# Routing one-hots stored with two tokens innermost, spilled activations read back into their ring ahead of use, gate table read in quarters

## The chip, the cores and the metric

The kernel runs on one NeuronCore of a Trainium2 chip. The metric is the device time of one execution, in microseconds (us). The kernel before takes 1592.83 us, the median of three runs between 1591.17 and 1601.28 us.

## What is computed

The reference is one decoder layer on 512 tokens of width 1024: attention and a convolution branch, then a retrieval layer ("PEER") over 16,384 single-neuron experts, then a gated embedding. The change lies in the PEER layer, whose core is:

```
def one_block(xb):
    q = (xb @ w_q).reshape(P, PEER_HEADS, 2, PEER_DK_HALF)
    s = jnp.einsum('phcd,hcnd->phcn', q, sub_keys).astype(jnp.float32)
    v1, i1 = lax.top_k(s[:, :, 0], PEER_TOPK)
    v2, i2 = lax.top_k(s[:, :, 1], PEER_TOPK)
    ...
    best, pos = lax.top_k(cand, PEER_TOPK)
    e = jnp.take_along_axis(cand_idx, pos, axis=-1)
    g = jax.nn.softmax(best, axis=-1)
    u = u_tab[e]
    act = jax.nn.gelu(jnp.einsum('pd,phkd->phk', xb, u).astype(jnp.float32), approximate=False)
    coef = (g * act).astype(xb.dtype)
    return jnp.einsum('phk,phkd->pd', coef, v_tab[e])
```

Each token chooses 8 x 16 = 128 of the 128 x 128 experts, each with a gate g. The expert number is i1 * 128 + i2.

## The kernel before

The 512 tokens are four groups of 128. The first group fetches its chosen experts' rows by indirect DMA (`gathered`: 128 rows of u, lines 802 and 806, then 128 rows of v, lines 813 and 816, each 512 KB for 128 tokens). The other three groups, 384 tokens, go through all 16,384 experts densely and are multiplied with a table of gates that is zero where an expert was not chosen. The dense work is 128 units of each of two kinds:

- An **A unit** e (`prep_act`, `dense_act`) loads 128 experts of u (tile `tr`, 512 KB), splits them into a high and a low part (`th` on ScalarE, `tl` on VectorE, the helper at lines 135 and 140), does 24 matmuls of 384 columns into `aps` (lines 148 to 150), and takes the GELU into a tile `act` from a ring of RING = 17. The activations of units 0 to 47 (e < SPILL) are written to memory (`ad`), the others stay in the ring.
- A **V unit** e (`prep_out`, `dense_out`) loads 128 experts of v (`tr` again), splits them, multiplies the activations with the gates into `cf` (VectorE, line 1020), splits `cf` into `ch` and `cl`, and does 18 matmuls of 512 columns into `vps`. The gates come from the table `gd` in memory, in chunks of GCH = 8 units: one DMA of 1.5 MB for each chunk, into `gch`, of which two buffers exist (`load_gates`, line 1008).

The order runs in stages. First 65 A units, during which VectorE finds the top keys of the four token groups (`topk`) and, for groups 1 to 3, builds the gate table (the scatter). Then 63 pairs of an A and a V unit, V in the order of `order`: units 48 to 127 first, whose activations are in the ring, then 0 to 47. Then 65 V units alone, the last 48 of which need an activation back from `ad` (tile `aback`, two buffers, loaded where the unit is prepared, line 1015). Units are prepared AHEAD = 2 units before they run; raw tiles `tr` have three buffers, split tiles four. The indirect DMAs and their VectorE work (`gj`, `acc`) are spread over all stages by a fixed rate.

The scatter of one group (`topk`'s end and `scatter`) makes, for every token, a matrix of 128 x 128 gates as a product: for each of the token's 128 choices (the partitions) a one-hot row of i1 and a one-hot row of i2 times the gate, contracted by TensorE. It goes by blocks of OCH = 8 tokens. VectorE compares a ramp `iok` with the indices `ids` (line 937, tile `o12`, the rows' `o`), giving both one-hots for 8 tokens in 2048 f16 elements, and multiplies the second by the gate's high and low half (line 944, `og`, 1024 elements each). TensorE then does two matmuls a token, stationary operand the first one-hot, moving operand `og`, 128 columns (lines 960 and 961, tile `gp`), and ScalarE writes four tokens at a time to `stg` (line 962), which SyncE (SP) stores into `gd`. In memory the tokens of a one-hot lie innermost, in runs of QUAD = 4, since VectorE reads and writes 16-bit elements that lie side by side:

```
o12 = ohp.tile([P, ng, 2, NK, QUAD], F16, name="o12", tag="o12")
nc.tensor.matmul(gp[:, i], o1[:, q // QUAD, :, i], og[:, 0, q // QUAD, :, i], start=True, stop=False)
```

So TensorE reads one token's 128 values at a step of four f16 elements, 8 bytes, in both operands, and VectorE reads the indices of a run (four elements, 8 bytes) once for each of the 128 values of the ramp. The one-hot tiles have two buffers each, and a scatter is issued LATE = 2 blocks after its one-hots.

SP issues nearly all the plain DMAs, in program order; a DMA that waits for a buffer holds those behind it.

Of the kernel before, what the change touches and what calls it, by code (L numbers as in the profile page):

```python
# [9 lines left out]
F32 = mybir.dt.float32  # L10
# [11 lines left out]
P = 128  # L22
# [27 lines left out]
WBUF = 4  # L50
EARLY = 65
# [3 lines left out]
QUAD = 4  # L55
# [38 lines left out]
def hymba_layer(ctx, tc, x, xT, p_t, pos, pvec, conv_ln_g, conv_ln_b, w_in, w_uq, w_ukv, w_out,  # L94
# [724 lines left out]
    with ExitStack() as fs:  # L819
# [9 lines left out]

        iok = mid.tile([P, NK, QUAD], F16, name="iok")  # L830
        nc.gpsimd.iota(iok, pattern=[[1, NK], [0, QUAD]], base=0, channel_multiplier=0,
                       allow_small_or_imprecise_dtypes=True)

        def topk(t):
# [83 lines left out]
            ids = ohp.tile([P, P // QUAD, 2, QUAD], F16, name="ids", tag="ids")  # L918
            nc.scalar.activation(ids, pt[:, 0:2].rearrange("p c (g q) -> p g c q", q=QUAD), AF.Copy)
# [9 lines left out]
            for c in range(P // TCH):  # L929
                stg = s8p.tile([P, NK, TCH], F32, name="stg", tag="s8")  # L930
                for c0 in range(0, TCH, OCH):
                    cs = slice(c * TCH + c0, c * TCH + c0 + OCH)
                    ng = OCH // QUAD
                    gs0 = cs.start // QUAD
                    o12 = ohp.tile([P, ng, 2, NK, QUAD], F16, name="o12", tag="o12")
                    og = ohp.tile([P, 2, ng, NK, QUAD], F16, name="og", tag="og")
                    nc.vector.tensor_tensor(
                        o12.rearrange("p g c n q -> p (g c) n q"),
                        iok.unsqueeze(1).to_broadcast([P, 2 * ng, NK, QUAD]),
                        ids[:, gs0:gs0 + ng].rearrange("p g c q -> p (g c) q").unsqueeze(2)  # L940
                        .to_broadcast([P, 2 * ng, NK, QUAD]), op=ALU.is_equal)
                    yield 1.2, 0.0
                    for part, gate in ((0, gh), (1, gl)):
                        nc.vector.tensor_tensor(  # L944
                            og[:, part], o12[:, :, 1],
                            gate[:, cs].rearrange("p (g q) -> p g q", q=QUAD).unsqueeze(2)
                            .to_broadcast([P, ng, NK, QUAD]), op=ALU.mult)
                    o1 = o12[:, :, 0]
                    late.append((c, c0, stg, o1, og))
                    if len(late) > LATE:  # L950
                        scatter(t, *late.pop(0))
                    yield 1.1, 0.94
# [3 lines left out]
        def scatter(t, c, c0, stg, o1, og):  # L956
            for q in range(0, OCH, QUAD):
                gp = ps_g.tile([P, 4, NK], F32, name="gp", tag="gp")
                for i in range(4):
                    nc.tensor.matmul(gp[:, i], o1[:, q // QUAD, :, i], og[:, 0, q // QUAD, :, i], start=True, stop=False)  # L960
                    nc.tensor.matmul(gp[:, i], o1[:, q // QUAD, :, i], og[:, 1, q // QUAD, :, i], start=False, stop=True)  # L961
# [34 lines left out]
    with ExitStack() as fs:  # L996
# [7 lines left out]
        def load_gates(c):  # L1004
            if len(gch) > 1:
                gch.pop(next(iter(gch)))
            gch[c] = cfp.tile([P, NTC, GCH, TCH], F32, name="gch", tag="gch")
            nc.sync.dma_start(gch[c].rearrange("p c n t -> p c (n t)"),
                              gd[:, :, c * GCH:(c + 1) * GCH, :].rearrange("c p n t -> p c (n t)"))

        def prep_out(e):
            stage(("V", e), v_tab.rearrange("(a b) d -> b a d", b=NK)[e], [P, D])
            if e < SPILL:
                a = cfp.tile([P, TD], F32, name="aback", tag="aback")
                nc.sync.dma_start(a, ad[e])
            else:
                a = acts.pop(e)
# [37 lines left out]
        def prep(u):  # L1055
# [4 lines left out]
            for j in (i, i + GCH - 1):  # L1060
                if j < NK and order[j] // GCH not in gch:
                    load_gates(order[j] // GCH)
# [174 lines left out]
```

## Time and profile before

| | |
|---|---|
| median of three runs | 1592.83 us |
| profiled execution, its time | 1598.58 us |
| its span in the trace | 1596.6 us |
| TensorE matmul (PE) busy | 1537.3 us, 96% |
| VectorE (DVE) busy | 1267.1 us, 79% |
| ScalarE (ACT) busy | 719.7 us, 45% |
| DMA | 386.54 MB, mean 242 GB/s |
| granted TensorE clock, mean | 0.983 |

The profiled execution is 5.75 us longer than the median of the three timed runs. Matmuls are pipelined: the record of one is as long as its passage through the array, so the time that it costs is read from one start to the next, and a busy PE may still be paced by something else. In the views, PE is the matmul, PEld the load of the stationary operand, DVE VectorE, ACT ScalarE, POOL GpSimd, SP SyncE; `L937` is line 937 of the kernel before. The helper's lines 135, 140 and 148 to 150 serve many tiles, so they are read by tile.

### The profile page before, as it was taken

To read this page: it belongs to the slowest core of one execution; us is meant where nothing else is said; L and a number is where in the kernel's file an instruction comes from. 1 tells how busy PE (TensorE), PEld (TensorE's weight loads), DVE (VectorE), ACT (ScalarE), POOL (GpSimd) and SP (SyncE) were. 2 spreads that over 40 slices of the span, in tenths; PEclk is the share of its full clock that TensorE was granted. 3 is DMA by queue.
4 is the path that set the end of the run, shared out by engine and by line. 5 is a ranking of instruction groups with operands and counts; after the bars stand their busy time and mean duration, and the time that the engine had idled before them with its cause. 6 is when DMAs were issued, how large, how long until landed. Compare 5 with 4: busy or idle time off the path is not lost.

```text
span 1596.6 us, 22808 instructions
## 1 busy us (share of the span) xinstructions
PE 1537.3 (96%) x8070; PEld 1361.4 (85%) x8070; DVE 1267.1 (79%) x2614; ACT 719.7 (45%) x1160; POOL 414.2 (26%) x302
## 2 busy tenths in 40 slices
PE   7999999999999999999999999899999999889997
PEld 6888777899899999999999998799988888768876
DVE  5999665699989899758879768697977966777766
ACT  6468864344564653653333323333332433333454
POOL 0000001000000001004545444464544543434100
PEclk9999989999999999999999999999999999999998
DMA  7321124436567666589989998898999899889842
GB/s 221 101 80 54 54 94 168 135 108 200 192 242 241 223 242 216 196 267 388 343 313 346 341 345 278 302 330 310 338 323 343 301 316 310 301 284 316 287 144 92
DMA packets 166913, 386.54 MB, mean 242 GB/s; under 512 B 12560, under 2 KB 81552, under 8 KB 163728
## 3 DMA queue, kind: packets, MB, share of 16 engines
q1 hardware_dynamic: 129360, 249.81, 45.9%
q0 software_dynamic: 36864, 134.23, 23.5%
q8 instruction: 63, 1.03, 0.3%
q10 hardware_dynamic: 576, 1.05, 0.2%
q14 instruction: 50, 0.41, 0.1%
HBM read 343.63 MB, written 41.42 MB: 241 GB/s over the span
## 4 chain that ended last, share of the span: by engine, by line
PE 51%; DVE 18%; DMA 16%; issue 8%; ACT 5%; POOL 2%; SPq 1%; DVEq 0%; POOLq 0%; ACTq 0%
PE aps L149 6%; PE aps L150 6%; PE aps L148 6%; PE vps L149 5%; PE vps L150 5%; PE vps L148 4%; DMA aback<-ad 4%; DVE tl L140 3%; DMA tr<-in_v_tab 3%; DMA gv<-in_v_tab,pidx 3%; DMA gu<-in_u_tab,pidx 3%; PE gp L960 3%; PE gp L961 3%; DVE cacc L304 2%; DMA tr<-in_u_t 2%
## 5 line engine op out<-in xcount | busy, mean ns | idle before, releaser
L135 ACT ACTIVATE th<-tr 128x1024 fp32r<-128x1024 f32 x256 | 270.7, 1058 | 475.4 <-DMA tr<-in_u_t 181.0
L140 DVE SCALAR_TENSOR_TENSOR tl<-tr,th 128x1024 fp32r<-128x1024 f32 x256 | 312.3, 1220 | 92.4 <-ACT th L135 91.3
L148 PE MATMUL aps<-mixh,th 128*128 128x384 f32 x1024 | 347.3, 339 | 1.9 <-ACT act L789 1.9
L150 PE MATMUL aps<-mixh,tl 128*128 128x384 f32 x1024 | 346.2, 338 | 0.0
L149 PE MATMUL aps<-mixl,th 128*128 128x384 f32 x1024 | 345.6, 338 | 0.0
L802 POOL DMA_INDIRECT gu<-in_u_tab,pidx x128 | 174.1, 1360 | 565.1 <-DVE gj L806 383.7
L149 PE MATMUL vps<-tl,ch 128*128 128x512 f32 x768 | 304.2, 396 | 11.6 <-DVE tl L140 11.5
L148 PE MATMUL vps<-th,ch 128*128 128x512 f32 x768 | 302.1, 393 | 6.9 <-ACT th L135 6.9
L150 PE MATMUL vps<-th,cl 128*128 128x512 f32 x768 | 302.8, 394 | 0.0
L813 POOL DMA_INDIRECT gv<-in_v_tab,pidx x128 | 213.9, 1671 | 249.6 <-DVE acc L816 217.8
L148 PEld LDWEIGHTS aps<-mixh,th 128*128 128x128 f32 x1024 | 193.8, 189 | 4.8 <-ACT act L789 2.3
L149 PEld LDWEIGHTS aps<-mixl,th 128*128 128x128 f32 x1024 | 193.5, 189 | 2.4
L150 PEld LDWEIGHTS aps<-mixh,tl 128*128 128x128 f32 x1024 | 193.4, 189 | 0.0
L149 PEld LDWEIGHTS vps<-tl,ch 128*128 128x128 f32 x768 | 145.8, 190 | 44.9 <-DVE tl L140 15.8
L806 DVE SCALAR_TENSOR_TENSOR gj<-gu,xn 128x1024 bf16<-128x1024 f32 x128 | 156.2, 1220 | 29.2 <-DMA gu<-in_u_tab,pidx 27.9
L148 PEld LDWEIGHTS vps<-th,ch 128*128 128x128 f32 x768 | 146.0, 190 | 37.6 <-ACT th L135 8.3
L816 DVE SCALAR_TENSOR_TENSOR acc<-gv,gact,acc 128x1024 f32<-128x1024 f32 x128 | 163.8, 1280 | 17.8 <-DMA gv<-in_v_tab,pidx 17.0
L150 PEld LDWEIGHTS vps<-th,cl 128*128 128x128 f32 x768 | 146.0, 190 | 30.5
L135 ACT ACTIVATE ch<-cf 128x384 fp32r<-128x384 f32 x128 | 66.6, 522 | 170.4 <-DVE cf L1020 79.6
L962 ACT ACTIVATE stg<-gp 128x512 f32<-128x512 f32 x96 | 95.4, 1106 | 50.2 <-PE gp L961 30.8
L960 PE MATMUL gp<-og,o 128*128 128x128 f16 x384 | 93.3, 296 | 1.2 <-DVE og L944 1.1
L961 PE MATMUL gp<-og,o 128*128 128x128 f16 x384 | 89.0, 296 | 0.6 <-DVE og L944 0.6
(301 smaller groups left out, 2230.9 us busy)
## 6 DMA issues: line engine op xcount, KB each, us to landing
tr<-in_u_t SPq DMA_DIRECT2D x128, 512.0 KB, 5.7
tr<-in_v_tab SPq DMA_DIRECT2D x128, 512.0 KB, 6.6
gd<-stg SPq DMA_DIRECT2D x24, 1024.0 KB, 4.8
gch<-gd SPq DMA_DIRECT2D x16, 1536.0 KB, 15.8
ad<-act SPq DMA_DIRECT2D x48, 192.0 KB, 3.9
aback<-ad SPq DMA_DIRECT2D x48, 192.0 KB, 5.6
wr<-in_gate_w SPq DMA_DIRECT2D x12, 512.0 KB, 3.3
wr<-in_w_out SPq DMA_DIRECT2D x8, 512.0 KB, 3.2
```

The costliest lines, as they stand in the source:

```text
L135: nc.scalar.activation(hi, src, AF.Copy)
L140: nc.vector.scalar_tensor_tensor(lo, src, 1.0 if g is None else g, hi.bitcast(F32), op0=ALU.mult, op1=ALU.subtract)
L148: nc.tensor.matmul(ps, lh, rh, start=first, stop=False)
L149: nc.tensor.matmul(ps, lh, rl, start=False, stop=False)
L150: nc.tensor.matmul(ps, ll, rh, start=False, stop=last)
L802: nc.gpsimd.indirect_dma_start(out=g, out_offset=None, in_=u_tab, in_offset=bass.IndirectOffsetOnAxis(ap=pidx[:, s:s + 1], axis=0))
L806: nc.vector.scalar_tensor_tensor(junk, g, 1.0, xn0, op0=ALU.mult, op1=ALU.mult, accum_out=gact[:, s:s + 1]))
L813: nc.gpsimd.indirect_dma_start(out=g, out_offset=None, in_=v_tab, in_offset=bass.IndirectOffsetOnAxis(ap=pidx[:, s:s + 1], axis=0))
L816: nc.vector.scalar_tensor_tensor(acc0, g, gact[:, s:s + 1], acc0, op0=ALU.mult, op1=ALU.add))
L960: nc.tensor.matmul(gp[:, i], o1[:, q // QUAD, :, i], og[:, 0, q // QUAD, :, i], start=True, stop=False)
L961: nc.tensor.matmul(gp[:, i], o1[:, q // QUAD, :, i], og[:, 1, q // QUAD, :, i], start=False, stop=True)
L962: nc.scalar.activation(stg[:, :, c0 + q:c0 + q + 4].rearrange("p n t -> p t n"), gp, AF.Copy, scale=1.0 / GSC)
```

## The change

It has two parts that touch different stages.

**Scatter.** QUAD = 4 becomes PAIR = 2. The ramp, the indices and the one-hots now have two tokens innermost: `o12` is [128, 4, 2, 128, 2] in place of [128, 2, 2, 128, 4], the same 2048 elements. The instructions are the same in number and size. TensorE's step between the values of a token becomes two f16 elements, 4 bytes; an index run that VectorE repeats along the ramp becomes two elements, 4 bytes.

**Gates and activations.** A chunk of gates is loaded by four DMAs of a quarter each (384 KB, six of the 24 token blocks), begun at four successive V units rather than by one DMA at the first of them. A spilled activation is loaded by `load_back` into a tile of the activation ring 16 V units before its own unit, rather than into one of two `aback` buffers at its own; `prep_out` then takes every activation from the ring.

```
+GPART = 4
...
-QUAD = 4
+PAIR = 2
...
-        iok = mid.tile([P, NK, QUAD], F16, name="iok")
-        nc.gpsimd.iota(iok, pattern=[[1, NK], [0, QUAD]], base=0, channel_multiplier=0,
+        iok = mid.tile([P, NK, PAIR], F16, name="iok")
+        nc.gpsimd.iota(iok, pattern=[[1, NK], [0, PAIR]], base=0, channel_multiplier=0,
...
-                    o12 = ohp.tile([P, ng, 2, NK, QUAD], F16, name="o12", tag="o12")
-                    og = ohp.tile([P, 2, ng, NK, QUAD], F16, name="og", tag="og")
+                    ng = OCH // PAIR
+                    gs0 = cs.start // PAIR
+                    o12 = ohp.tile([P, ng, 2, NK, PAIR], F16, name="o12", tag="o12")
+                    og = ohp.tile([P, 2, ng, NK, PAIR], F16, name="og", tag="og")
                     nc.vector.tensor_tensor(
                         o12.rearrange("p g c n q -> p (g c) n q"),
-                        iok.unsqueeze(1).to_broadcast([P, 2 * ng, NK, QUAD]),
+                        iok.unsqueeze(1).to_broadcast([P, 2 * ng, NK, PAIR]),
                         ids[:, gs0:gs0 + ng].rearrange("p g c q -> p (g c) q").unsqueeze(2)
-                        .to_broadcast([P, 2 * ng, NK, QUAD]), op=ALU.is_equal)
+                        .to_broadcast([P, 2 * ng, NK, PAIR]), op=ALU.is_equal)
...
-                    nc.tensor.matmul(gp[:, i], o1[:, q // QUAD, :, i], og[:, 0, q // QUAD, :, i], start=True, stop=False)
-                    nc.tensor.matmul(gp[:, i], o1[:, q // QUAD, :, i], og[:, 1, q // QUAD, :, i], start=False, stop=True)
+                    g, r = divmod(q + i, PAIR)
+                    nc.tensor.matmul(gp[:, i], o1[:, g, :, r], og[:, 0, g, :, r], start=True, stop=False)
+                    nc.tensor.matmul(gp[:, i], o1[:, g, :, r], og[:, 1, g, :, r], start=False, stop=True)
...
-        def load_gates(c):
-            if len(gch) > 1:
-                gch.pop(next(iter(gch)))
-            gch[c] = cfp.tile([P, NTC, GCH, TCH], F32, name="gch", tag="gch")
-            nc.sync.dma_start(gch[c].rearrange("p c n t -> p c (n t)"),
-                              gd[:, :, c * GCH:(c + 1) * GCH, :].rearrange("c p n t -> p c (n t)"))
+        def load_gates(c, part):
+
+            if part == 0:
+                if len(gch) > 1:
+                    gch.pop(next(iter(gch)))
+                gch[c] = cfp.tile([P, NTC, GCH, TCH], F32, name="gch", tag="gch")
+            n = NTC // GPART
+            cs = slice(part * n, (part + 1) * n)
+            nc.sync.dma_start(gch[c][:, cs].rearrange("p c n t -> p c (n t)"),
+                              gd[cs, :, c * GCH:(c + 1) * GCH, :].rearrange("c p n t -> p c (n t)"))
+
+        def load_back(e):
+
+            acts[e] = actp.tile([P, TD], F32, name="aback", tag="act")
+            nc.sync.dma_start(acts[e], ad[e])
...
-            if e < SPILL:
-                a = cfp.tile([P, TD], F32, name="aback", tag="aback")
-                nc.sync.dma_start(a, ad[e])
-            else:
-                a = acts.pop(e)
+            a = acts.pop(e)
...
-            for j in (i, i + GCH - 1):
-                if j < NK and order[j] // GCH not in gch:
-                    load_gates(order[j] // GCH)
+            for part in range(GPART):
+                if i == 0:
+                    load_gates(order[0] // GCH, part)
+                j = i + GCH - 1 - part
+                if j % GCH == 0 and GCH <= j < NK:
+                    load_gates(order[j] // GCH, part)
+            j = i + RING - 1
+            if NK - SPILL <= j < NK:
+                load_back(order[j])
```

On PE and ACT the order of the instructions is the same before and after. On VectorE it differs in three places, where a `cf` moves ahead by a few instructions. The order on SP differs throughout the stages with V units. There, `tr` is a raw tile of weights, `gch` a gate chunk, `aback` an activation read back from `ad`; the numbers tell buffers apart.

SP at the last gate chunk of the pair stage, before:

```order
L773 DMA tr_12451<-in_u_t 128x1024
L1008 DMA gch_12670<-gd_3279 128x24x128
L773 DMA tr_12487<-in_v_tab 128x1024
L773 DMA tr_12523<-in_u_t 128x1024
L773 DMA tr_12559<-in_v_tab 128x1024
```

The same place in the change:

```order
L774 DMA tr_12478<-in_u_t 128x1024
L1014 DMA gch_12699<-gd_3279 128x6x128 x2
L774 DMA tr_12514<-in_v_tab 128x1024
L1014 DMA gch_12699<-gd_3279 128x6x128 x2
L774 DMA tr_12550<-in_u_t 128x1024
```

One V unit's weights have moved between the two halves of the chunk; the next A unit's weights still come behind all of it.

SP in the V-only stage, at a gate chunk, before:

```order
L1015 DMA aback_13454<-ad_3280 128x384
L773 DMA tr_13448<-in_v_tab 128x1024
L1008 DMA gch_13483<-gd_3279 128x24x128
L773 DMA tr_13485<-in_v_tab 128x1024
L1015 DMA aback_13491<-ad_3280 128x384
L773 DMA tr_13520<-in_v_tab 128x1024
L1015 DMA aback_13526<-ad_3280 128x384
```

In the change, at the first chunk after the start of the V-only stage:

```order
L774 DMA tr_12951<-in_v_tab 128x1024
L1020 DMA aback_12949<-ad_3280 128x384
L1014 DMA gch_12984<-gd_3279 128x6x128 x2
L1020 DMA aback_12986<-ad_3280 128x384
L774 DMA tr_12988<-in_v_tab 128x1024
L1014 DMA gch_12984<-gd_3279 128x6x128 x2
L1020 DMA aback_13022<-ad_3280 128x384
L774 DMA tr_13024<-in_v_tab 128x1024
```

The chunk is in two halves there as well, and the activations beside it are those of units 16 later. The first five returns stand together behind the sixth weight tile of the V-only stage; before, the returns (but for the first two) began behind the 20th.

## Rows read from the trace of the kernel before

**Rows 1.** Busy us (instructions): PE, PEld, DVE, ACT, POOL; clock, DMA share, GB/s
```profile
331.00:411.00 80.00, 76.42 (x452) 75.31 (x451) 79.71 (x387) 37.24 (x53) 3.96 (x4) 1.00 0.53 173
411.00:477.00 66.00, 64.15 (x442) 58.58 (x442) 57.64 (x112) 41.42 (x47) 2.30 (x2) 0.97 0.64 224
...
518.00:583.00 65.00, 65.00 (x455) 61.12 (x454) 55.78 (x98) 41.13 (x48) 3.03 (x3) 1.00 0.64 230
...
630.00:699.00 69.00, 69.00 (x472) 64.38 (x471) 53.21 (x67) 43.55 (x52) 3.45 (x3) 0.98 0.60 213
699.00:1248.00 549.00, 541.50 (x2729) 492.12 (x2728) 431.60 (x555) 189.01 (x262) 260.33 (x184) 0.99 0.93 328
1248.00:1533.00 285.00, 274.00 (x1181) 223.99 (x1180) 206.37 (x256) 100.68 (x135) 104.91 (x53) 0.98 0.85 294
```

**Rows 2.** Timeline of PE: start us, us, engine, line, operation
```profile
308.82 0.28 PE L149 MATMUL sps<-kbl,pqh 128*128 128x256 f32 x1
...
310.02 0.28 PE L150 MATMUL sps<-kbh,pql 128*128 128x256 f32 x1
```

**Rows 3.** The same view, an A unit, then a scatter
```profile
654.28 0.33 PE L148 MATMUL aps<-mixh,th 128*128 128x384 f32 x1
...
655.49 0.34 PE L149 MATMUL aps<-mixl,th 128*128 128x384 f32 x1
...
656.38 0.30 PE L960 MATMUL gp<-og,o 128*128 128x128 f16 x1
...
657.69 0.30 PE L960 MATMUL gp<-og,o 128*128 128x128 f16 x1
```

**Rows 4.** Waits of 699 to 1533 us: total us, times, longest
```profile
DVE cf L1020 <- DMA aback<-ad: 55.4, 15, 9.4
...
PE vps L149 <- DVE tl L140: 11.5, 9, 4.2
...
PE vps L148 <- ACT th L135: 6.9, 3, 4.4
```

**Rows 5.** The chain that ended last, start us, us, what; around one PE gap
```profile
1348.20 10.22 DMA aback<-ad
```

**Rows 6.** Timeline of PE, the same gap: [idle before <- releaser]
```profile
1361.92 0.50 PE L149 MATMUL vps<-tl,ch 128*128 128x512 f32 x1 [2.53 <-DVE tl L140]
```

**Rows 7.** By line: duration ns min/median/max, first and last start us, forms
```profile
L960 PEld LDWEIGHTS <-o x384: 113/117/139, 413.6 to 697.9; 128*128 128x128 f16 x192
L497 PEld LDWEIGHTS <-identb x32: 96/98/152, 110.7 to 217.3; 128*128 128x128 bf16 x32
L670 PEld LDWEIGHTS bank<-identf,xt x32: 138/140/144, 265.2 to 277.0; 128*128 128x128 f32 x32
L670 PE MATMUL bank<-identf,xt x32: 270/272/273, 265.4 to 277.1; 128*128 128x128 f32 x32
```

**Rows 8.** Timeline of PE, eight transposes one behind the other
```profile
265.43 1.03 PE L670 MATMUL bank<-identf,xt 128*128 128x128 f32 x8
```

**Rows 9.** DVE groups by form: xcount | busy us, mean ns | idle before, releaser
```profile
L140 DVE SCALAR_TENSOR_TENSOR tl<-tr,th 128x1024 fp32r<-128x1024 f32 x256 | 312.3, 1220 | 92.4 <-ACT th L135 91.3 <-PE vps L150 0.8
L140 DVE SCALAR_TENSOR_TENSOR cl<-cf,ch 128x384 fp32r<-128x384 f32 x128 | 70.6, 551 | 5.5 <-ACT ch L135 5.4
L937 DVE TENSOR_TENSOR o<-iok,ids 128x2048 f16<-128x2048 f16 x48 | 58.3, 1218 | 19.1 <-PE gp L961 18.8
L944 DVE TENSOR_TENSOR og<-o,gl 128x1024 f16<-128x1024 f16 x48 | 32.7, 682 | 0.0
...
L840 DVE TENSOR_TENSOR cand<-tv 128x448 f32<-128x448 f32 x4 | 2.4, 609 | 0.0
```

**Rows 10.** DMA issues of 1248 to 1533 us: xcount, KB each, us to landing
```profile
gch<-gd SPq DMA_DIRECT2D x6, 1536.0 KB, 15.1
aback<-ad SPq DMA_DIRECT2D x46, 192.0 KB, 5.5
...
gv<-in_v_tab,pidx POOLq DMA_INDIRECT x52, 8.1
```

More of the change, by code (lines that the diff above doesn't have):

```diff
@@ L917, in topk @@
             nc.tensor.transpose(pt[:, 2], pg, identf)
-            ids = ohp.tile([P, P // QUAD, 2, QUAD], F16, name="ids", tag="ids")
-            nc.scalar.activation(ids, pt[:, 0:2].rearrange("p c (g q) -> p g c q", q=QUAD), AF.Copy)
+            ids = ohp.tile([P, P // PAIR, 2, PAIR], F16, name="ids", tag="ids")
+            nc.scalar.activation(ids, pt[:, 0:2].rearrange("p c (g q) -> p g c q", q=PAIR), AF.Copy)
             gh = ohp.tile([P, P], F16, name="gh", tag="gh")
@@ L932, in topk @@
                     cs = slice(c * TCH + c0, c * TCH + c0 + OCH)
-                    ng = OCH // QUAD
-                    gs0 = cs.start // QUAD
-                    o12 = ohp.tile([P, ng, 2, NK, QUAD], F16, name="o12", tag="o12")
-                    og = ohp.tile([P, 2, ng, NK, QUAD], F16, name="og", tag="og")
+                    ng = OCH // PAIR
+                    gs0 = cs.start // PAIR
+                    o12 = ohp.tile([P, ng, 2, NK, PAIR], F16, name="o12", tag="o12")
+                    og = ohp.tile([P, 2, ng, NK, PAIR], F16, name="og", tag="og")
                     nc.vector.tensor_tensor(
                         o12.rearrange("p g c n q -> p (g c) n q"),
-                        iok.unsqueeze(1).to_broadcast([P, 2 * ng, NK, QUAD]),
+                        iok.unsqueeze(1).to_broadcast([P, 2 * ng, NK, PAIR]),
                         ids[:, gs0:gs0 + ng].rearrange("p g c q -> p (g c) q").unsqueeze(2)
-                        .to_broadcast([P, 2 * ng, NK, QUAD]), op=ALU.is_equal)
+                        .to_broadcast([P, 2 * ng, NK, PAIR]), op=ALU.is_equal)
                     yield 1.2, 0.0
@@ L945, in topk @@
                             og[:, part], o12[:, :, 1],
-                            gate[:, cs].rearrange("p (g q) -> p g q", q=QUAD).unsqueeze(2)
-                            .to_broadcast([P, ng, NK, QUAD]), op=ALU.mult)
+                            gate[:, cs].rearrange("p (g q) -> p g q", q=PAIR).unsqueeze(2)
+                            .to_broadcast([P, ng, NK, PAIR]), op=ALU.mult)
                     o1 = o12[:, :, 0]
@@ L956, in scatter @@
         def scatter(t, c, c0, stg, o1, og):
-            for q in range(0, OCH, QUAD):
+            for q in range(0, OCH, 4):
                 gp = ps_g.tile([P, 4, NK], F32, name="gp", tag="gp")
                 for i in range(4):
-                    nc.tensor.matmul(gp[:, i], o1[:, q // QUAD, :, i], og[:, 0, q // QUAD, :, i], start=True, stop=False)
-                    nc.tensor.matmul(gp[:, i], o1[:, q // QUAD, :, i], og[:, 1, q // QUAD, :, i], start=False, stop=True)
+                    g, r = divmod(q + i, PAIR)
+                    nc.tensor.matmul(gp[:, i], o1[:, g, :, r], og[:, 0, g, :, r], start=True, stop=False)
+                    nc.tensor.matmul(gp[:, i], o1[:, g, :, r], og[:, 1, g, :, r], start=False, stop=True)
                 nc.scalar.activation(stg[:, :, c0 + q:c0 + q + 4].rearrange("p n t -> p t n"), gp, AF.Copy,
```

## The prediction

> **What bounds the kernel now.** I read the table of busy time by stretch first [rows 1], since the two parts of the change lie in different stages. The stage of 65 A units runs from 331 to 699 us. The three scatters lie in it at 411 to 477, 518 to 583 and 630 to 699 us; between them VectorE finds the top keys and is busy all the time (79.71 of 80 us in the first such stretch), so nothing that TensorE gains can be used there. In the scatters it is the other way round: TensorE is busy for 64 to 69 us of each, and VectorE for 57.64, 55.78 and 53.21 us. VectorE's slack in them is 8.4 + 9.2 + 15.8 = 33.4 us. Where it stood idle before a compare, it mostly waited for the scatter's matmuls to free a one-hot buffer, 18.8 us in all [rows 9]. So TensorE sets the time of the scatters.
>
> A busy PE says little of its pace, so I read that from starts in the timeline. In the key scores, ten matmuls of 256 columns start between 308.82 and 310.02 us, 120 ns each [rows 2]. In an A unit, seven of 384 columns start between 654.28 and 655.49 us, 173 ns each [rows 3]. These two give 53 / 128 = 0.41 ns a column and 14 ns fixed, so 128 columns should take 67 ns. In a scatter, eleven steps of 128 columns lie between 656.38 and 657.69 us, 119 ns each [rows 3]. That is the pace of 256 columns. Something doubles the cost of these 768 matmuls: either the moving operand is read at half speed, or the load of the stationary operand takes that long.
>
> From 699 us on the list of waits says where TensorE lost time: 11.5 us for `tl` and 6.9 us for `th`, so 18.4 us [rows 4]. The granted clock adds to it: 0.99 over 549 us and 0.98 over 285 us [rows 1] are 5.5 + 5.7 = 11.2 us at which the array stood at the lower level or returned to the upper one after such gaps. Together 29.6 us. One gap shows the mechanism: a returned activation, issued at 1348.20 us, is on the chain for 10.22 us [rows 5], VectorE waits in order for it before `cf`, the next `tl` is late, and TensorE stands idle for 2.53 us until 1361.92 us [rows 6]. VectorE spent 55.4 us in waits of that kind [rows 4]. A gate chunk of 1536 KB takes 15.1 us to land, an activation of 192 KB behind it 5.5 us in the median [rows 10].
>
> **Part one, the scatter.** No instruction is added or removed: 48 compares, 96 multiplications, 768 matmuls and as many loads of the same sizes.
>
> TensorE: the step of both operands falls from 8 bytes to 4, which is the step of the f32 operands of the A units and key scores, read at full pace [rows 2, 3]. So the moving operand should no longer bind, and the low end is 67 ns a matmul. The high end is today's 119 ns; a slower one I exclude, since the 4-byte step is that of nearly every matmul in the kernel. Between them stands the load. A load of f32 for transposes lasts 138 to 140 ns [rows 7], while the transposes follow each other at (1030 - 272) / 7 = 108 ns [rows 7, 8], so 32 ns of a load overlap the next one. The shortest f16 load of the scatter lasts 113 ns, one of contiguous bf16 98 ns [rows 7]. Less 32 ns, these can be repeated every 81 and 66 ns. I take 81, the nearer to a stepped f16 operand. Then TensorE saves 38 ns x 256 = 9.7 us in a scatter. VectorE's slack caps it: 8.4 + 9.2 + 9.7 = 27.3 us. With two buffers for each one-hot tile the two engines will not fit together without gaps; I keep three quarters, 20.5 us. The ends are nothing at 119 ns and 8.4 + 9.2 + 13.3 = 31 us at 67 ns. If only the load's 108 ns of the f32 case were reached, it would be 11 ns x 768 = 8 us.
>
> [...]
>
> VectorE: a compare takes 1218 ns for 2048 elements, a multiplication 682 ns for 1024 [rows 9]. At f32, 1024 elements take 1220 ns and 384 take 551 [rows 9], so 1.05 ns an element and 150 ns fixed; the one-hots run at two elements in that time. The change makes the repeated run one 4-byte word instead of two. The nearest row is the candidate sum of line 840, where one f32 word is read eight times in a row: 609 ns for 448 elements [rows 9], and the two rows above give 618. Reading the same word again cost nothing there, so I take no change. The other end is the loss of the doubled rate: 2290 and 1220 ns, so 1.07 + 2 x 0.54 = 2.15 us a block and 103 us over 48 blocks.
>
> **Part two, gates and activations.** The bytes are the same. SP issues 48 more DMAs for gates (64 for 16), and the returns, 48 as before, start behind the sixth weight tile of the V-only stage in place of the 20th. Each is issued some 16 units, 16 x 18 x 226 ns = 65 us, before its use, against a landing of 5.5 us [rows 10], so VectorE's 55.4 us of waiting for them should go. What a return waits for is the buffer of the unit before, a `cf` that is older than the `tl` for which the weight tile behind it waits anyway, so it holds nothing back on SP. What comes late next is a weight tile or a gathered row, for the DMA is nearly full. A V unit alone takes 18 x 226 ns = 4.07 us and needs 512 + 192 + 1536 / 8 KB, and with 52 gathers in about 55 units another 0.95 x 512 KB: 1.41 MB, or 347 GB/s. The stretch moved 294 GB/s at a share of 0.85 [rows 1], so about 346 at 1. So I take half of the 29.6 us in the profiled execution, 15 us. In the pair stage the halves of a chunk let one V tile pass earlier, while the A tile still stands behind the whole chunk, which is another reason for half. The ends: nearly all of it, and a loss. The loss: returns now travel in the first 14 V-only units too, which had nearly none; 14 x 192 KB are 2.75 MB or 8 us at 346 GB/s.
>
> **The sum.** Profiled execution: 1598.6 - 20.5 - 15 = 1563 us. It stands 5.75 us above the median of the shown runs, which spread over 10 us; what varies is most likely the same waits, so the median has 29.6 - 5.75 = 24 us of them, and half is 12 us. Median: 1592.8 - 20.5 - 12 = 1560, which I put at 1561.
>
> **The rivals.**
>
> *VectorE loses the doubled rate* (slower). At one element in the time of two, the compares and multiplications add 103 us against a slack of 33.4 us; the scatters, then bound by VectorE, grow by 70 us, and with part two the time is 1592.8 + 70 - 12 = 1651 us. It decides from 33.4 / 48 = 0.7 us a block on, that is, when a block's 2.58 us become 3.3. Against it stands line 840; for it only that no row has 16-bit pairs repeated. [...]
>
> *The scatter's pace stays between 108 and 119 ns*, because the load binds. Part one gives 0 to 8 us: 1573 to 1581, say 1577 us. For it speaks that f32 loads without any step already repeat at only 108 ns; against it, that the f16 loads are 25 ns shorter.
>
> *The DMA is the bound of the V-only stage*, and the waits move from returns to weights and gathers, with 8 us more at its start: 1592.8 - 20.5 + 8 = 1580 us. For it speaks the demand of 347 against 346 GB/s; against it, that the weights have three raw and four split buffers and the returns 16 units of reserve.
>
> *Neither part does what it says*: about 1593 us.
>
> **How the numbers follow.** Forecast 0.50, pace unchanged 0.24, DMA-bound 0.12, VectorE at half rate 0.08, nothing 0.06. The forecast's own range takes 12 to 31 us of part one and 6 to 22 us of part two: 1540 to 1575. The range of 1543 to 1588 holds nearly all of it and of the second and third rival, 0.81; it leaves out the slower rival, nothing at all, and tails. About 1%, 16 us, is what a measurement of this kernel can tell from no change: 1577 and 1609 us. Faster: the forecast, half of the unchanged pace and a little of the DMA case, 0.63. Slower: 0.08 and 0.01 of unforeseen, 0.09. Within 1%: 0.28.
>
> **What would show it.** In the profile of the changed kernel the starts of `gp` matmuls should lie about 81 ns apart; 108 or more proves the second rival. The compare should stay at 1218 and the multiplication at 682 ns; 1.9 or 2.3 us for the compare is the first rival. The three scatters should shorten to 58 to 62 us each, with VectorE busy for 86 to 97% of them. VectorE's wait for `aback` should be gone, and TensorE's waits behind 699 us be about 9 us; if they are 18 again, with `th` waiting for weights and a DMA share near 1 between 1248 and 1440 us, it is the third. The prediction is wrong as a whole if the A stage does not shorten though the pace falls, which would mean that VectorE, not TensorE, set the scatters.

## The result, and the profile after

The changed kernel takes 1553.15 us, the median of four runs between 1550.69 and 1557.0 us, against 1593.67 us for the kernel before beside it (1591.17 to 1601.28). The ratio is 0.975, with a 95% interval from 0.971 to 0.979. Forecast were 1561 us and a range from 1543 to 1588. The profiled execution took 1550.69 us, with a span of 1548.7 us and a mean granted clock of 0.99.

The two profiled executions differ by 47.9 us, the medians by 40.5: the profiled execution of before is 4.9 us above its median, that of the change 2.5 us below. I cut both spans at the first matmul of an A unit, the first of a V unit, the last of an A unit and the last of a V unit, by their starts in the timeline:

| stage, us | before | after | forecast in the sum | measured |
|---|---|---|---|---|
| ahead of the A units | 334.7 | 331.8 | 0 | -2.9 |
| 65 A units, top keys, scatters | 384.0 | 352.8 | -20.5 | -31.2 |
| 63 pairs of an A and a V unit | 527.0 | 528.2 | -15 with the next | +1.2 |
| V units alone | 287.1 | 273.6 | | -13.5 |
| behind the V units | 63.8 | 62.3 | 0 | -1.5 |

The first and the last stage hold nothing that was changed. Over all the runs below they lie between 331 and 335 and between 62 and 64 us, so these two move by 4 and 2 us by themselves.

The same stretches as in [rows 1], by busy time of each engine (PE, PEld, DVE, ACT, POOL, with instructions in brackets), granted clock, DMA share and GB/s:

```profile
409.00:466.00 57.00, 54.16 (x459) 48.91 (x457) 56.97 (x112) 41.75 (x49) 2.29 (x2) 0.97 0.77 270
506.00:562.00 56.00, 55.83 (x479) 51.85 (x479) 55.49 (x98) 42.89 (x50) 3.77 (x3) 0.99 0.77 278
609.00:666.00 57.00, 56.88 (x476) 52.26 (x475) 52.15 (x65) 42.49 (x50) 3.44 (x3) 0.97 0.73 256
666.00:1215.00 549.00, 539.33 (x2717) 486.95 (x2716) 429.40 (x553) 187.39 (x262) 263.30 (x183) 1.00 0.93 327
1215.00:1487.00 272.00, 270.05 (x1190) 222.38 (x1189) 208.40 (x258) 100.67 (x135) 101.37 (x54) 1.00 0.89 311
```

The first three lines are the scatters, now 57, 56 and 57 us instead of 66, 65 and 69. Their third figure is VectorE: it is busy all the time in the first two, where it had 8.4 and 9.2 us of slack. The fourth line is the pair stage, the fifth that of V units alone.

The scatter's pace, in the timeline of TensorE as in [rows 3] (start us, us of one, engine, line); then the loads of its stationary operand as in [rows 7] (duration ns min/median/max, first and last start us):

```profile
657.39 0.22 PE L962 MATMUL gp<-og,o 128*128 128x128 f16 x1
...
658.08 0.22 PE L963 MATMUL gp<-og,o 128*128 128x128 f16 x1
```

```profile
L962 PEld LDWEIGHTS <-o x384: 96/97/144, 410.7 to 663.9; 128*128 128x128 f16 x192
...
  DVE og L945: 9.4, 36
```

Twelve steps from one start to the next lie between 657.39 and 658.08 us, 57 ns each, where it was 119. A load still lasts 97 ns, longer than the matmul's turn; loads lie over one another. The last line says what TensorE (loads and matmuls together) waits for ahead of line 962: VectorE's products, 9.4 us in 36 waits. The wait has changed sides.

VectorE's groups as in [rows 9] (busy us, mean ns | idle before):

```profile
L938 DVE TENSOR_TENSOR o<-iok,ids 128x2048 f16<-128x2048 f16 x48 | 57.9, 1215 | 0.1
...
L945 DVE TENSOR_TENSOR og<-o,gl 128x1024 f16<-128x1024 f16 x48 | 32.7, 681 | 0.0
L1027 DVE TENSOR_TENSOR cf<-aback,gch 128x384 f32<-128x384 f32 x48 | 26.4, 550 | 0.2
```

The compare and the product cost what they did, 1215 and 681 ns. The idle time ahead of the compare, 19.1 us before, is 0.1. Ahead of `cf` with a returned activation VectorE stands idle for 0.2 us in all; before, its waits for `aback` were 55.4 us [rows 4].

The waits behind 666 us (us in total, times, longest) and the DMA issues from 1215 to 1487 us (KB each, median us to landing), as in [rows 4] and [rows 10]:

```profile
ACT th L136 <- DMA tr<-in_u_t: 258.2, 53, 9.2
...
PE vps L150 <- DVE tl L141: 7.3, 11, 1.0
...
PE vps L149 <- ACT th L136: 1.7, 2, 1.1
PE aps L149 <- ACT act L790: 1.6, 3, 0.7
...
PE aps L151 <- DVE tl L141: 1.0, 4, 0.3
```

```profile
aback<-ad SPq DMA_DIRECT2D x48, 192.0 KB, 6.8
gch<-gd SPq DMA_DIRECT2D x24, 384.0 KB, 10.3
```

TensorE's own waits, the lines that begin with PE, are 11.6 us where those of before were 18.4. A return lands 6.8 us after its issue, a quarter of a chunk 10.3. ScalarE waits for the weights of most A units of the pair stage: 258.2 us in 53 waits, up to 9.2 us each. That is no new wait, but a longer one. Before, from 699 to 1533 us:

```profile
ACT th L135 <- DMA tr<-in_u_t: 177.8, 49, 9.1
```

The weights come just in time or a little late, as they did, and the stage of pairs has gained nothing.

### The profile page after: what moved, and what is told of

It reads as the page before. It is cut to its first block, busy times and chain, and to the rows that moved or that the text cites. A ratio compares the mean times of both kernels' runs of the same rounds, so it can differ in the third digit from the quotient of the medians.

```text
span 1548.7 us, 22818 instructions
## 1 busy us (share of the span) xinstructions
PE 1490.1 (96%) x8070; PEld 1314.2 (85%) x8070; DVE 1263.9 (82%) x2614; ACT 715.5 (46%) x1160; POOL 414.6 (27%) x302
## 4 chain that ended last, share of the span: by engine, by line
DMA 20%; issue 15%; PE 10%; DVE 6%; POOL 5%; ACT 2%; SPq 0%; POOLq 0%; DVEq 0%; ACTq 0%
DMA gu<-in_u_tab,pidx 8%; DMA gv<-in_v_tab,pidx 7%; PE vps L150 3%; PE vps L151 3%; PE vps L149 3%; DMA tr<-in_v_tab 3%; POOL gv L814 3%; POOL gu L803 2%; DMA tr<-in_u_t 1%; DVE tl L141 1%; DVE gj L807 1%; DVE acc L817 1%; DVE cf L1027 1%; ACT th L136 1%; DVE cl L141 1%
## 5 line engine op out<-in xcount | busy, mean ns | idle before, releaser
L150 PE MATMUL vps<-tl,ch 128*128 128x512 f32 x768 | 301.1, 392 | 7.3 <-DVE tl L141 7.3
L138 ACT ACTIVATE wh<-wr,pv 128x512 fp32r<-128x512 f32 (+2 forms) x84 | 55.1, 694 | 53.2 <-PE bank L151 25.8
L141 DVE SCALAR_TENSOR_TENSOR cl<-cf,ch 128x384 fp32r<-128x384 f32 x128 | 70.5, 551 | 8.2 <-ACT ch L136 8.2
## 6 DMA issues: line engine op xcount, KB each, us to landing
gch<-gd SPq DMA_DIRECT2D x64, 384.0 KB, 10.2
```

Source lines behind the costliest of these rows:

```text
L138: nc.scalar.activation(hi, src, AF.Copy, scale=g)
L141: nc.vector.scalar_tensor_tensor(lo, src, 1.0 if g is None else g, hi.bitcast(F32), op0=ALU.mult, op1=ALU.subtract)
L150: nc.tensor.matmul(ps, lh, rl, start=False, stop=False)
```

## The experiments

Four questions: do the two parts add up, and what of part two brings its gain; which operand made the scatter slow; why the pair stage gave nothing; and what sets the A stage now. All kernels differ from the kernel before or after only by what is shown ("..." marks lines left out). Median times with a ratio come from three rounds beside the kernel before; a time without one is a single profiled run.

### The two parts alone

`e1_pair_only` is the changed kernel with the gate loads and the returns of the kernel before. `e2_gates_only` is the changed kernel with four tokens innermost again:

```
 e1:
-        def load_gates(c, part):
...
+        def load_gates(c):
...
-            a = acts.pop(e)
+            if e < SPILL:
+                a = cfp.tile([P, TD], F32, name="aback", tag="aback")
+                nc.sync.dma_start(a, ad[e])
+            else:
+                a = acts.pop(e)
...
 e2:
-PAIR = 2
+PAIR = 4
```

> Part one alone: two tokens innermost, gates and returned activations as before. Theory (the parts add up, and part one is worth the 30 us by which the three scatters shortened): 1562 to 1566 us against 1594 before, three scatters of 57, 56 and 57 us, the V-only stage as before at 285 us. Rival (the parts help each other, so that part one alone is bound later by the same waits): 1572 us or more. In either case scatter matmuls 57 ns apart.

> Part two alone: four tokens innermost as before, gates in quarters and early returns. Theory: 1580 to 1584 us (12 us of the V-only stage, nothing in the pair stage), scatters as before at 66, 65 and 69 us. Rival (part two needs the earlier end of the A stage): within 4 us of before. Other rival (part two is worth the 24 us that the waits cost): 1570 us.

The first took 1564.06 us, ratio 0.980 (0.977 to 0.984), the second 1581.27, ratio 0.990 (0.987 to 0.993). Both lie where their theories put them. Of `e1_pair_only`, waits behind 666 us:

```profile
DVE cf L1022 <- DMA aback<-ad: 52.7, 13, 9.8
...
PE vps L150 <- DVE tl L141: 13.1, 10, 2.6
```

The stage of A units is 353.0 us, as short as with both parts, and VectorE still waits 52.7 us for returned activations; V units alone take 285.3 us as before. In `e2_gates_only` it is the mirror image: 384.1 and 271.9 us. So part one is the A stage and part two the V stage, and they nearly add: 0.980 x 0.990 = 0.970, just below the interval of 0.971 to 0.979 for both.

### The two edits of part two, each with part one

`e3_pair_quarters` keeps the quarters and drops the early returns; `e4_pair_back` keeps the early returns and loads whole chunks:

```
 e3, and prep_out as in e1, load_back left out:
-            if NK - SPILL <= j < NK:
-                load_back(order[j])
```

```
 e4, and load_gates as in e1:
-            for part in range(GPART):
...
+            for j in (i, i + GCH - 1):
+                if j < NK and order[j] // GCH not in gch:
+                    load_gates(order[j] // GCH)
```

> Part one and the gates in quarters, the activations returned at their own unit into two buffers as before. Theory (the early returns bring the V-only gain): like part one alone, 1562 to 1566 us, V-only stage 283 to 286 us, VectorE waiting about 50 us for returns. Rival (it is the quarters that bring it, since one chunk of 1.5 MB in front of the returns made them late): 1552 to 1555 us, V-only stage 272 us.

> Part one and the early returns, the gates in one DMA a chunk as before. Theory (the early returns bring the V-only gain): 1552 to 1556 us, V-only stage 272 us, no wait of VectorE for returns. Rival (the quarters bring it): 1562 to 1566 us, V-only stage 283 us with TensorE gaps some 15 to 20 us behind each gate DMA.

The quarters alone took 1550.2 us, ratio 0.971 (0.968 to 0.975); the early returns alone 1556.47, ratio 0.975 (0.972 to 0.978). Neither can be told from both together (0.975, 0.971 to 0.979). For the quarters my theory missed and its rival was right, but for 2 us at its lower end; for the early returns the theory held (1552 to 1556 us). The waits of the quarters behind 666 us:

```profile
DVE cf L1026 <- DMA aback<-ad: 40.5, 18, 5.6
...
PE vps L150 <- DVE tl L141: 7.1, 9, 1.3
```

The early returns:

```profile
PE vps L149 <- ACT th L136: 3.4, 2, 2.3
...
PE vps L150 <- DVE tl L141: 2.8, 5, 0.8
```

In `e3_pair_quarters` VectorE still waits 40.5 us for returned activations, 18 times. But the longest such wait is 5.6 us and no longer 9.4, and V units alone take 273.6 us as with both edits. That fits a reserve of split tiles which outlasts the shorter waits; it is argued from these lengths, not tested. `e4_pair_back` has no wait for returns, and its V units take 276.2 us, in a profiled execution (1546.13 us) that is 10 us below its median. So the loss needed two things at once: 1.5 MB of gates in one piece, and an activation behind it that is wanted right away. Taking away either gets most of it back, and the second removal adds nothing that these runs can tell.

### Which operand made the scatter slow

Three kernels vary the step, one the width of VectorE's run. `e5_moving_flat` reads only the moving operand as 128 values that lie side by side, `e6_weights_flat` only the stationary one; both read other values than the reference needs, in the same amount, so their results are wrong. `e7_step16` has eight tokens innermost, `e11_one_token` one.

```
 e5, with PAIR = 4 (the second matmul likewise):
-                    nc.tensor.matmul(gp[:, i], o1[:, g, :, r], og[:, 0, g, :, r], start=True, stop=False)
+                    nc.tensor.matmul(gp[:, i], o1[:, g, :, r], og[:, 0, g, :32].rearrange("p n q -> p (n q)"), start=True, stop=False)
 e6, with PAIR = 4 (the second matmul likewise):
+                    nc.tensor.matmul(gp[:, i], o1[:, g, :32].rearrange("p n q -> p (n q)"), og[:, 0, g, :, r], start=True, stop=False)
 e7:
+PAIR = 8
 e11:
+PAIR = 1
```

> The kernel before with four tokens innermost and its own gate loads and returns, but the scatter's matmuls read their moving operand as 128 f16 that lie side by side (the stationary operand keeps its step of 8 bytes). The number and size of all instructions is unchanged; the gate columns that are read are the wrong ones, so the gates of the dense part are not the reference's. Theory: the moving operand's step of 8 bytes set the pace of 119 ns. Then the gp matmuls start 57 to 67 ns apart, their loads stay at 113 to 117 ns, and the stage of A units shortens by about 31 us as with two tokens innermost: 1560 to 1566 us in all. Rival: the load of the stationary operand with its step set the pace. Then the matmuls stay 110 to 119 ns apart and the time at 1590 to 1598 us.

> The mirror image: four tokens innermost, the moving operand keeps its step of 8 bytes, and the stationary operand is read as 128 f16 that lie side by side. The rows of gates that come out are the wrong ones, so the gates of the dense part are not the reference's. Theory (the moving operand sets the pace): the loads fall from 113 to about 97 ns each, the matmuls stay 110 to 119 ns apart and the time stays at 1590 to 1598 us. Rival (the load sets the pace): matmuls 57 to 81 ns apart and 1560 to 1575 us. If both kernels with one flat operand stay at 119 ns, either operand alone is enough to bind.

> The kernel before with eight tokens innermost instead of four, so that both operands are read at a step of 16 bytes, and an index run is eight f16. Theory: the pace of a matmul goes with the bytes between its elements beyond 4 (57 ns at 4, 119 at 8), so 128 columns take 220 to 240 ns; 768 matmuls by some 110 ns lengthen the scatters by about 85 us, to 1665 to 1690 us. Rival: the pace has two levels only, full at 4 bytes and half beyond, so the matmuls stay at 110 to 125 ns and the time at 1590 to 1600 us. For both the compares stay at 1218 and the multiplications at 682 ns.

> The changed kernel with one token innermost instead of two: both operands of the scatter's matmuls lie side by side, and an index run that VectorE repeats is a single f16. Theory: VectorE then loses the rate of two 16-bit elements at a time, a compare takes about 2290 and a multiplication 1220 ns, a block 2.15 us more; 48 blocks lengthen the scatters, which VectorE sets already, by 103 us, to 1645 to 1660 us, while the matmuls stay 55 to 57 ns apart. Rival: only the elements that are written and the ramp have to lie side by side, the compare stays at 1215 and the multiplication at 681 ns, and the time at 1548 to 1556 us.

The first three were built on the changed kernel and so carry part two, unlike what their expectations say. Their times are to be compared with the 1581.27 us of `e2_gates_only`, and the forecasts in them to be lowered by some 12 us.

They took 1556.05, 1578.22, 1712.53 and, for `e11_one_token`, 1654.12 us. The A stage is 352.8 us in `e5_moving_flat`, as in the changed kernel, and 380.9 in `e6_weights_flat`, 3 us less than in `e2_gates_only`. The matmuls and loads of the scatter, `e5_moving_flat` first (the load's line as above; then the timeline):

```profile
L962 PEld LDWEIGHTS <-o x384: 111/113/148, 412.2 to 665.5; 128*128 128x128 f16 x192
```

```profile
659.00 0.22 PE L962 MATMUL gp<-og,o 128*128 128x128 f16 x1
...
659.67 0.22 PE L963 MATMUL gp<-og,o 128*128 128x128 f16 x1
```

`e6_weights_flat`:

```profile
L962 PEld LDWEIGHTS <-o x384: 95/115/126, 409.8 to 691.0; 128*128 128x128 f16 x192
```

```profile
682.21 0.30 PE L962 MATMUL gp<-og,o 128*128 128x128 f16 x1
...
683.60 0.29 PE L963 MATMUL gp<-og,o 128*128 128x128 f16 x1
```

`e7_step16`:

```profile
821.06 0.42 PE L962 MATMUL gp<-og,o 128*128 128x128 f16 x1
...
822.23 0.41 PE L963 MATMUL gp<-og,o 128*128 128x128 f16 x1
```

The steps between starts: 12 in 0.67 us with the moving operand flat, 56 ns each; 12 in 1.39 us with the stationary one flat, 116 ns; 5 in 1.17 us at a step of 16 bytes, 234 ns. At a step of 8 bytes the moving operand alone set the pace. In `e5_moving_flat` the loads, at a step of 8 bytes, last 113 ns and matmuls still follow each other every 56: a load that is twice as long as the turn of a matmul hid beneath it. In `e6_weights_flat` the loads did not fall to 97 ns as I had expected; that part missed. Each doubling of the step beyond 4 bytes about doubled the time of the 128 columns (57, then 116 to 119, then 234 ns), and from 4 bytes to 2 it gained 1 ns. At 4 and at 16 bytes both operands have the step, so there the two are not told apart.

With eight tokens innermost the A stage is 517.6 us instead of the 384.1 of `e2_gates_only`, which is 133 us more, not the 768 x 115 ns = 88 us of the columns; the expected time, too, was missed by over 30 us. The rest shows in the granted clock (stretches as above, second scatter):

```profile
570.00:680.00 110.00, 110.00 (x450) 87.83 (x449) 57.43 (x138) 43.49 (x47) 3.02 (x3) 0.75 0.38 139
```

TensorE is recorded busy for the whole 110 us, and the granted clock is 0.75. The 256 matmuls of the scatter at 234 ns are 60 us of it; the 194 of A units take the other 50, 258 ns each where 173 is their pace. Between scatter matmuls nine steps of an A unit take 320 ns each, 1.85 times that pace:

```profile
599.86 0.53 PE L149 MATMUL aps<-mixh,th 128*128 128x384 f32 x1
...
602.74 0.53 PE L149 MATMUL aps<-mixh,th 128*128 128x384 f32 x1
```

In the trace of before, behind the gap of [rows 6], steps of 512 columns take 427 ns between 1363.23 and 1365.79 us, at a granted clock of 0.50, and 226 ns ahead of the gap, at 1.00: a factor of 1.89. So I estimate the clock of these nine steps at about 0.50.

`e11_one_token`, VectorE's groups:

```profile
L938 DVE TENSOR_TENSOR o<-iok,ids 128x2048 f16<-128x2048 f16 x48 | 109.0, 2292 | 9.1 <-PE gp L963 9.1
...
L945 DVE TENSOR_TENSOR og<-o,gl 128x1024 f16<-128x1024 f16 x48 | 58.8, 1224 | 0.0
```

With a single f16 repeated along the ramp VectorE lost its doubled rate, 2292 and 1224 ns instead of 1215 and 681, though the ramp and the output lie side by side. The kernel takes 101 us more than the changed one, as expected. So of the widths 1, 2, 4 and 8 the run of two is the only one at which both engines have the best rate that these runs show: TensorE had it at a step of 2 and 4 bytes (56 and 57 ns a matmul), VectorE at runs of 4, 8 and 16 bytes (1215, 1218 and 1223 ns a compare).

### Why the pair stage gave nothing

Between 838 and 850 us the changed kernel's SP issues these DMAs, at the gate chunk of that place (timeline of SP: start us, us):

```profile
840.75 0.33 SPq L774 DMA_DIRECT2D tr<-in_u_t  x1
841.21 1.09 SPq L1014 DMA_DIRECT2D gch<-gd  x2
842.71 1.91 SPq L774 DMA_DIRECT2D tr<-in_v_tab  x1
844.66 3.92 SPq L1014 DMA_DIRECT2D gch<-gd  x2
848.68 4.45 SPq L774 DMA_DIRECT2D tr<-in_u_t  x1
```

The program text puts the four quarters at four successive V units; in the order that came out on SP they are joined into two halves with one V tile between, and the weights of the next A unit stand behind all 1.5 MB. About 20 us later TensorE stands still (timeline of PE, [idle before <- releaser]):

```profile
864.04 0.44 PE L149 MATMUL aps<-mixh,th 128*128 128x384 f32 x1 [0.71 <-ACT act L790]
864.93 0.44 PE L151 MATMUL aps<-mixh,tl 128*128 128x384 f32 x1 [0.26 <-DVE tl L141]
870.09 0.50 PE L150 MATMUL vps<-tl,ch 128*128 128x512 f32 x1 [0.84 <-DVE tl L141]
879.25 0.50 PE L150 MATMUL vps<-tl,ch 128*128 128x512 f32 x1 [0.58 <-DVE tl L141]
```

Such gaps stand behind the five later chunks of the stage as well; behind the two before it, at 705 and 771 us, there are none. Over the 549 us TensorE is idle for 9.7 us, where it was 7.5 [rows 1]: the halves have not taken the gaps away. `e8_gates_in_order` holds the quarters where the text has them; the order on VectorE and TensorE is unchanged. `e10_in_order_jit` does that too, but with the activations read back as in `e3_pair_quarters`.

```
-            nc.sync.dma_start(gch[c][:, cs].rearrange("p c n t -> p c (n t)"),
-                              gd[cs, :, c * GCH:(c + 1) * GCH, :].rearrange("c p n t -> p c (n t)"))
+            tc.keep_in_program_order(
+                nc.sync.dma_start(gch[c][:, cs].rearrange("p c n t -> p c (n t)"),
+                                  gd[cs, :, c * GCH:(c + 1) * GCH, :].rearrange("c p n t -> p c (n t)")))
```

> The changed kernel, with the four quarters of a gate chunk held in the place in which the program text puts them, one at each of four V units, instead of two halves on SP. Theory: the small gaps of TensorE some 20 us behind every chunk of the pair stage (0.4 to 2 us, about 14 us in all) come from the half chunks, that is 768 KB ahead of an A unit's weights; with a quarter there they shrink, the pair stage goes from 528 to 520 to 523 us and the time to 1542 to 1548 us. Rival: the gaps come from the DMA being nearly full there, whatever the size of a piece; the pair stage stays at 526 to 530 us and the time at 1548 to 1555 us.

> The kernel with the quarters kept in order, but with the activations read back as in the kernel before, at their own unit and into two buffers. Theory: with the quarters spread, no returned activation stands behind more than 384 KB of gates, so the early return is worth nothing more: the stage of V units alone stays at 269 to 271 us and the time at 1531 to 1537 us. Rival: the early return still brings its share, VectorE waits for activations hold TensorE, that stage takes 274 us or more, and the time is 1538 to 1546 us.

The first took 1533.37 us (1530.79 to 1536.17), ratio 0.963 (0.959 to 0.967), which is below the interval of the changed kernel; the second 1533.88, ratio 0.960 (0.955 to 0.965). The first beat its theory by 9 us, the second fell where its theory put it. Of `e8_gates_in_order`, SP at such a place, and the stretches and waits behind the A stage:

```profile
877.54 0.33 SPq L774 DMA_DIRECT2D tr<-in_u_t  x1
877.92 0.43 SPq L1015 DMA_DIRECT2D gch<-gd  x1
879.61 0.33 SPq L774 DMA_DIRECT2D tr<-in_v_tab  x1
884.22 0.33 SPq L774 DMA_DIRECT2D tr<-in_u_t  x1
```

```profile
666.00:1203.00 537.00, 537.00 (x2730) 490.63 (x2729) 440.50 (x562) 192.43 (x266) 277.83 (x186) 1.00 0.96 339
1203.00:1470.00 267.00, 267.00 (x1179) 221.15 (x1179) 204.08 (x249) 96.81 (x133) 82.01 (x50) 1.00 0.89 308
```

```profile
ACT th L136 <- DMA tr<-in_u_t: 19.6, 7, 5.4
```

Each A unit's weights now stand behind at most one quarter, 384 KB. ScalarE's wait for them falls from 258.2 us in 53 waits to 19.6 in 7. TensorE is busy for all of 804 us at a clock of 1.00. The pair stage takes 514.8 us, the V stage 269.3. The DMA moves more a second than before, 339 GB/s at a share of 0.96, and TensorE never waits for it: what cost the time was the order of its work, not its rate. The gain does not hang on one execution. The pair stage takes 521.6 to 531.4 us in the ten kernels whose gates come whole or in halves (the kernel before among them), and 514.8 to 514.9 in the three whose quarters stand apart (this one and the two below). That 53 units waited in the changed kernel, and not only those next to a chunk, fits a stock of weights that is used up behind one chunk and hardly comes back, since the stage runs near what the DMA delivers; this last step is argued, not shown.

In `e10_in_order_jit`, with activations read at their own unit (its stretch of V units, and VectorE's wait):

```profile
1205.00:1470.00 265.00, 265.00 (x1172) 219.38 (x1171) 204.54 (x249) 97.03 (x133) 83.40 (x50) 1.00 0.89 305
```

```profile
DVE cf L1027 <- DMA aback<-ad: 9.7, 10, 2.0
```

TensorE is busy all the time there too. With the quarters in their places the early return is worth nothing that these runs can tell.

### Does VectorE alone set the A stage now?

`e9_six_early` is `e8_gates_in_order` with fewer gathered rows in the A stage:

```
-G_EARLY = 18
+G_EARLY = 6
```

> The kernel with the quarters kept in order (1533.4 us), but with 6 gathered rows instead of 18 in the stage of 65 A units; the other 12 move into the stages with V units. Theory: VectorE sets the A stage now, so it loses 12 multiplications of 1.22 us and shortens by 12 to 15 us (352 to about 338), and the later stages stay at their pace although their DMA share of 0.96 rises: 1517 to 1523 us. First rival: the DMA has nothing left there; 12 x 512 KB more at 346 GB/s are 18 us, TensorE waits for weights again, and the time comes out at 1530 to 1540 us. Second rival: something else sets the A stage, which stays at 350 us: 1530 to 1536 us.

It took 1530.67 us (1529.38 to 1532.13), ratio 0.959 (0.954 to 0.963). That can't be told from the 1533.37 us that it starts from; the theory missed. Its first scatter and its pair stage:

```profile
409.00:466.00 57.00, 52.39 (x432) 47.70 (x431) 56.14 (x106) 39.67 (x46) 1.15 (x1) 0.91 0.73 250
...
690.00:1205.00 515.00, 515.00 (x2600) 468.18 (x2599) 437.40 (x562) 182.16 (x251) 274.66 (x192) 1.00 0.97 348
```

The first rival falls: the DMA takes the 12 gathers at a share of 0.97 in the pair stage, and TensorE is busy for all 515 us of it. But the A stage is 348.7 us, only 3 us shorter, although 12 products of 1.22 us have left it and VectorE is busy for 323.9 us of it instead of 334.7. In the first scatter TensorE now stands idle for 4.6 us and its clock is 0.91, where `e8_gates_in_order` has 3.1 us and 0.97. The second rival is the one that is left: VectorE does not set the stage alone. The two engines take turns in this run: from 329 to 562 us VectorE is busy for 231 of 233 us, from 562 to 666 us TensorE for 103.5 of 104.

The edit also does more than its line says. G_EARLY enters the rate at which A units and the routing on VectorE are interleaved, and the first two scatters begin behind 18 and 36 A units instead of 17 and 35. So the run does not show what the 12 products cost by themselves, and what sets the stage is not settled. TensorE's own work there is 1584 matmuls of A units (the 65 and the first of the pairs) at 173 ns and 768 of the scatter at 57, 318 us together with nothing else. Of the 31 us beyond that TensorE is idle for 10.7; the rest stays open.

## Why the prediction was right, and where it was not

The time fell into the range, on the side below the forecast, and the forecast was the right case. Step by step:

- **The scatter was paced by TensorE**: right. The three scatters shortened by 9, 9 and 12 us (58 to 62 us had been forecast for each, 56 and 57 came), and the A stage is as short when only this part is made (`e1_pair_only`).
- **The pace, 81 ns**: wrong, 57 was measured, below the low end of 67. Two steps failed. I took the load for what would bind next, by its duration less an overlap of 32 ns; `e5_moving_flat` shows a turn of 56 ns with loads of 113 ns. There the duration of a load was no bound on how often one can start. And the 14 ns fixed that I drew from f32 matmuls did not hold for f16: 128 columns at the 0.41 ns of [rows 2, 3] are 53 ns, so 4 of the 57 are left.
- **VectorE's slack as the cap, and three quarters of it**: the slack of 33.4 us was the cap (at 81 ns only 27.3 of it counted), and the factor was wrong. 31.2 us were gained, 0.93 of the slack: VectorE is busy for 56.97 of 57 and 55.49 of 56 us in the first two scatters, and for 52.15 of 57 in the third. The buffers, two of each one-hot, did not stop it. The factor and the pace lacked about as much each.
- **VectorE keeps its rate**: right. 1215 and 681 ns, as line 840 had said [rows 9], so the first rival fell. `e11_one_token` puts the bound next to it: one f16 alone costs 2292 ns, the price that I gave for the loss (2290). One 4-byte word that is read again cost nothing: 1215 ns where two words in turn took 1218.
- **The second rival**, a pace that stays at 108 to 119 ns, fell with the 57 ns. Of the two causes that the prediction left open, the load or the moving operand, it was the moving operand: at its step of 8 bytes a matmul took 119 ns with the stationary operand stepped and 116 with it flat, at 4 bytes in both 57.
- **Part two, 12 us of the median**: right in size; `e2_gates_only` is 1.0% faster, some 15 us, and the V stage of the changed kernel 13.5 us shorter. The half that I took of the loss came from no row, so that the size came out is luck. The step behind it was half wrong. The early return that I named as the cure was enough but not needed; the quarters without it gave the same. TensorE's waits fell to 11.6 us, where I had about 9. And I had set against the loss of 29.6 us half of it, as if each stage could give some; the pair stage gave nothing, and all the gain came from the V stage.
- **The pair stage**: the prediction saw in the recorded order that the A tile still stands behind the whole chunk and priced it as "another reason for half". That place in the order was worth 18 us: both stages together took 814.1 us before and 801.8 after, and take 784.1 in `e8_gates_in_order`. Those 30 us are about the loss of 29.6 us that the prediction had counted; that they agree so closely is chance, since a clock of 0.99 over 549 us is known only to some 3 us.
- **The third rival**, the DMA as the bound of the V stage: fell. Demand and rate are near each other as worked out, but the same bytes pass at a share of 0.96 and 0.89 without one wait of TensorE once the quarters stand apart.

## What to carry to other kernels

Ask of every strided TensorE operand whether it is the moving one, and at what step: here 4 bytes in both operands cost 57 ns where 2 in the moving one cost 56, 8 in the moving one 116 and 16 in both 234, while the stationary operand's step of 8 bytes cost no time at all (56 ns with the moving one flat). A layout between two engines can have a window, and here it was one width wide: two tokens innermost, 57 ns a matmul and 1215 ns a compare, between 2292 ns a compare at one token and 119 ns a matmul at four; test the widths on both sides. And where the DMA is nearly full, here at a share of 0.93, look at the recorded order of its queue before you shrink or advance transfers: the halves of a chunk, with one V tile between them, left the pair stage at 528.2 us where the whole chunk had 527.0, and here it was worth 18 us to set the quarters apart.

## What the runs showed of the hardware that I had not expected

- A matmul's turn went with the step of its operands: 56 ns with the moving one at 2 bytes, 57 with both at 4, 116 with the moving one at 8 and 234 with both at 16, for 128 columns of f16. At 8 bytes it was the moving operand's step: with the stationary one flat 116 ns, with both stepped 119. Loads of 113 ns passed beneath a turn of 56.
- TensorE was recorded busy without a gap and still granted less: 0.75 over the 110 us of a scatter at 234 ns a matmul (`e7_step16`), 1.00 over the 65 us of the second scatter in [rows 1] at 118 ns (31 steps from 539.83 to 543.49 us).
- The recorded time of a load did not go with its own operand's step alone: with the stationary operand flat and the moving one at 8 bytes it still lasted 115 ns in the median, with both at 4 bytes 97.
- The DMA ran at a share of 0.97 and 348 GB/s over the 515 us of the pair stage in `e9_six_early`, and TensorE was busy for all of them.
